# Head norms' squares joined in pairs before they are summed, key roots as two parts, and the second half's x kept unshifted: a hybrid decoder block on one core

## The chip, the cores and the metric

The kernel runs on one core of a Trainium2 chip. The metric is the device time of a run in microseconds; the time of a kernel is the median of its runs. TensorE is called PE, VectorE DVE, ScalarE ACT, GpSimd POOL and SyncE SP, as in the profile.

## The reference, cut to what matters

x has 2048 tokens by 1024 channels, in float32. Twelve heads of 128 channels in three groups (dilations 1, 4 and 16) attend over a banded window of at most 128 earlier keys.

```python
h = rms_norm(x, norm_w) * (1.0 + scale) + shift          # shift, scale, gate from silu(c) @ w_ada + b_ada
a, b, g_conv, q, k, v, g_attn, m_conv, m_attn = split(h @ w_in)
u = depthwise_causal_conv(a * sigmoid(b), conv_w, conv_b)      # 31 taps
y_conv = (silu(layer_norm(u)) * silu(g_conv)) @ w_conv_out
q = rope(rms_norm(q, q_norm_w), positions)               # per head of 128
k = rope(rms_norm(k, k_norm_w), positions)
o = softmax-weighted sum over the three groups of dilated_window_attention(q, k, v)
y_attn = (o * silu(g_attn)) @ w_attn_out
y = sigmoid(m_conv) * y_conv + sigmoid(m_attn) * y_attn
x = x + gate * (y @ w_out)
```

The part that the change touches most is `rms_norm` of the heads: the mean of the squares of each head's 128 channels, its inverse root, and the product with q or k.

## The kernel before, in words

**Products.** The combined projection is done in two halves of 1024 tokens. Each product of two 2 x 2 blocks is formed from seven block products (Strassen's scheme, names A11, S1 to S4 for the activations, B11, T1 to T4 for the weights). Each operand is split into a high and a low part of reduced precision (F32R), and a block product is twelve matmuls of 128 x 512 (`product`, line 311): three for each of four slices of 128 channels.

**Slots.** One block product is one slot. `slots` lists them in order: the values of the first pairs, then the q, k, v quads of seven slots each, then the gates' and the convolution's quads, and all this again for the second half. The first half's q, k, v stage lies at about 100 to 345 us of the profile with the attention trailing it, its gates and convolution at 590 to 1010 us, the second half's q, k, v stage at about 1080 to 1510. Work beside the products hangs on an agenda: `at_slot(s, f, where)` puts it into slot s, at the places "enter", "load", "act", "pe", "vec", "act2", (the products, with "mid" after the sixth of twelve) "tail" and "store", in this order. On PE, DVE, ACT, POOL and SP the order of instructions is the order of the program, so an instruction that waits holds up all behind it on its engine. Weight loads are asked five slots ahead, their splits done three slots ahead (`prepare`, lines 248 and 249; subtractions of weights on POOL, line 243).

**A rotation** (`rotate`) belongs to a pair of heads of q or of k: 12 for q and 12 for k in all, each on two registers `reg[0]` and `reg[1]` (the two halves of the heads' channels, 128 rows, two column halves c of 512 tokens). e4, e5, e6 are the slots of the quad's fifth to seventh product. ACT squares the four pieces (line 588); PE sums each over its channels with four products with the selector `sel`, one in each group of 32 columns of the array (line 601, four calls of `sums`, the two of one c adding up in PSUM); ACT adds eps (line 607); PE turns the rows into columns (line 612); ACT copies 16 columns (line 617); POOL takes the power -0.5 (line 621). For q the roots go into the scores' mask step. For k ACT widens them (line 631, two steps of 128 x 512), PE spreads them by eight products with the identity (line 638), DVE multiplies k by them (line 642), and SP stores (line 647). Meanwhile DVE turns by the positions' angles, twelve steps (lines 658 to 665).

**Attention** (`unit`) runs in units of two blocks of 128 queries, one every second slot, after its q, k, v are stored: scores (line 764), the mask step on DVE (line 776), exponents, transposed probabilities (line 792), values (line 817). The first half's attention waits for the end of the second half's x.

**The second half's x** (`later_load`, `later_scale`, `later_sum`) is normed beside the first half's q, k, v stage: loaded, multiplied by its row roots (DVE, line 1282), scaled and shifted in place (ACT, line 1283), summed in Strassen's combinations (DVE, line 1291), and stored; `quarter_split` (line 183) splits it when the second half starts. How its steps fall on slots is set by `busy`, `room` and `when`.

**The start** (lines 994 to 1200): x's first rows are squared and summed on PE, the modulation is formed from c and w_ada (`ada_mm`, `ada_mod`), `first_part` scales, shifts and splits x, and `angle_steps` works through the positions' angles on DVE.

Of the kernel before, what the change touches and what calls it, by code (L numbers as in the profile page):

```python
# [62 lines left out]
def tile_hybrid_block(  # L63
# [79 lines left out]
    nc.gpsimd.memset(eps, EPS)  # L143
    hpool_c = [tc.tile_pool(name=f"hT{i}", bufs=1, side="right", reuse_waits="tile") for i in range(2)]
# [67 lines left out]
    def rope_open(half):  # L212
        p = opened(rp, pool("rp"))
        rp["cos"], rp["sin"] = (p.tile([P, HS], F32, name=f"{n}{half}") for n in ("cos", "sin"))

# [347 lines left out]
    def turn_v(half, _, u0, g, reg, n, at):  # L563
        s0 = at[6]
# [13 lines left out]
    def rotate(half, which, u0, g, reg, n, at):  # L578
# [12 lines left out]
        turns = []  # L591

        def sums(c, i):
            def f():
                if not turns:
                    box["pr"] = bank("u", f"pss{n}")
                pr, sq = box["pr"], box.pop(("sq", c, i))
                first, done = not turns, c in turns
                turns.append(c)
                for q in range(4):  # L600
                    nc.tensor.matmul(pr[32 * q : 32 * q + 32, P * c : P * c + P], sel, sq[:, P * q : P * q + P],
                                     start=first, stop=done, skip_group_check=True)
            return f
# [5 lines left out]
        def turned():  # L609
            pt = box["pt"] = bank("t", f"prq{n}")  # L610
            for c in range(2):
                nc.tensor.transpose(pt[:, P * c : P * c + P], box["rows"][:, c], ident)

        def more():
            st = box["st"] = rb["p"].tile([P, 32], F32, tag="st", name=f"st{n}", bufs=2)
            got = box["pt"][:, : 2 * P].rearrange("p (c q m) -> p c q m", c=2, q=4)[..., :2]
            nc.scalar.activation(st[:, :16].rearrange("p (c q m) -> p c q m", c=2, q=4), got, AF.Copy)
# [8 lines left out]

        def widen():
            box["wide"] = rp["p"].tile([P, 16, 64], F32, tag="wide", name=f"rw{n}", bufs=1)
            for c in range(2):
                sl = slice(8 * c, 8 * c + 8)  # L630
                nc.scalar.activation(box["wide"][:, sl], box["st"][:, 16 + 8 * c : 24 + 8 * c][:, :, None].to_broadcast([P, 8, 64]), AF.Copy)

        def spread():
            box["rs"] = [bank("tu"[c], f"rs{n}_{c}") for c in range(2)]
            for c in range(2):
                for q in range(4):
                    w = box["wide"][:, 8 * c + 2 * q : 8 * c + 2 * q + 2].rearrange("p m r -> p (m r)")
                    nc.tensor.matmul(box["rs"][c][:, P * q : P * q + P], w, ident, start=True, stop=True)
# [36 lines left out]
        for s, c, i in sq:  # L675
            at_slot(s, square(c, i), "act" if s > e6 else "act2")
            at_slot(max(s, e6 - 1), sums(c, i), "tail")
        ops = rope()
        assert sum(count) == 12
        for d, k in enumerate(count):  # L680
            rope_slots[start + d] = k
            for _ in range(k):
                at_slot(start + d, lambda: next(ops)())
        end = start + len(count)
        at_slot(last, rows, "act")
        at_slot(last, turned, "mid")
        at_slot(last, more, "tail")
        at_slot(last + 1, roots)
# [3 lines left out]
        else:  # L692
            at_slot(last + 2, widen, "act2")
            at_slot(last + 2, spread, "tail")
            for c in range(2):
                for i in range(2):
                    at_slot(last + 3 + c, key_scale(c, i))
            assert last + 3 + 1 >= end - 1
            for i in range(2):
                at_slot(last + 5, store(i), "load")  # L700
# [3 lines left out]
    def unit(half, u, bs, state):  # L704
# [18 lines left out]
        def load():  # L723
# [25 lines left out]
            state["prev"] = own[1]  # L749
            box["q"] = [qk[:, 0, i] for i in range(2)]  # L750
# [106 lines left out]
    wide = su.tile([P, KC, 32], F32, name="wide")  # L857
# [56 lines left out]
    def ada_mm(g, acc, k):  # L914
        for q in range(4):
            nc.tensor.matmul(acc[32 * q : 32 * q + 32, :256], wide[:, k], landed_ada(g, k)[:, q // 2, 256 * (q % 2) : 256 * (q % 2) + 256],
# [25 lines left out]
    def first_part(name, k, t):  # L942
# [59 lines left out]
    nc.vector.tensor_copy(wide, sc[:, :, None].to_broadcast([P, KC, 32]))  # L1002
# [145 lines left out]
    angle_steps(3)  # L1148
# [54 lines left out]
    at_slot(1, lambda: angle_steps(3))  # L1203
# [49 lines left out]
    def later_root():  # L1253
        nc.vector.tensor_tensor(xst1[:, 16:24], xst1[:, :8], xst1[:, 8:16], op=ALU.add)
        rsqrt_cols(xst1[:, 24:32], xst1[:, 16:24], 8, xst1[:, 32:40])

# [22 lines left out]
    def later_scale(k, i):  # L1279
        name, kh, t = LATER[i]  # L1280
        kk, q = 4 * kh + k, xh[name]
        nc.vector.tensor_tensor(q, q, xh["rs"][:, 512 * t : 512 * t + 512], op=ALU.mult)
        nc.scalar.activation(q, q, AF.Identity, scale=mod[:, KC + kk : KC + kk + 1], bias=mod[:, kk : kk + 1])
# [3 lines left out]
    def later_sum(k, n, dst, x0, x1, op):  # L1287
# [3 lines left out]
        nc.vector.tensor_tensor(*q, op=op)  # L1291
# [13 lines left out]
    for w in ((Q, 0), (K, 0), (Q, 1), (K, 1), (Q, 2), (K, 2)):  # L1305
        g = GROUPS[2 * w[1] // NH]
        s6 = slots_of[0, *w][6]
        busy.update(range(s6 + (2 if g == 2 else 0), s6 + (7 if g == 2 else 6)))
# [6 lines left out]
    for k in range(4):  # L1315
# [3 lines left out]
        for args in ((3, "s3", "11", "21", ALU.subtract), (1, "21", "21", "22", ALU.add), (2, "11", "21", "11", ALU.subtract),  # L1319
                     (4, "12", "12", "11", ALU.subtract)):  # L1320
            work.append(lambda k=k, args=args: later_sum(k, *args))
# [3 lines left out]
        when += 2  # L1325
# [48 lines left out]
    for half in range(2):  # L1374
        for pair in range(6):
# [6 lines left out]
            ready = max(k6 + (11 if g == 2 else 10), v6 + 7, free_at[half])  # L1382
# [11 lines left out]
        at_slot(q_end + 6, lambda half=half: conv_open(half), "enter")  # L1394
# [531 lines left out]
```

## Time and profile before

| | |
|---|---|
| median of three runs | 2396.64 us (2391.16 to 2396.83) |
| profiled execution, its own time | 2400.4 us |
| its span, first to last instruction | 2398.6 us |
| PE busy | 2319.5 us (97%) |
| DVE busy | 1751.2 us (73%) |
| ACT and POOL busy | 1093.7 us (46%), 1083.1 us (45%) |
| mean granted TensorE clock | 0.986 |

How to read the profile: busy times are per engine; a line number is a line of the kernel before; "out<-in" names what an instruction writes and reads, numbers of buffers left out; "<-" in brackets names what ended the idle time before an instruction. A full-precision product is recorded as two matmuls, so x16 is eight products. A matmul's duration includes its way through the array, so the distance between starts, 0.23 us for 128 x 512, is what it costs in a run. In a timeline row the first number is the start in us, the second the duration.

### The profile page before, as it was taken

Reading aid. Unit: us, or ns where it says so; the run is one execution under the profiler, and the core shown is the slowest. Engines: PE = TensorE matmul, PEld = TensorE weight load, DVE = VectorE, ACT = ScalarE, POOL = GpSimd, SP = SyncE. Lnnn points to the kernel's source line nnn. Section 1 sums busy time; section 2 is a strip of 40 time slices with the busy share of each in tenths; the row PEclk is TensorE's granted clock in tenths of the full one; section 3 lists DMA queues with packets and bytes.
Section 4 is the critical chain, followed back from the end, with each engine's and each line's share of the span. In section 5 each row is a group of like instructions: output and inputs, shape, how many; then the busy total and the mean of one; then the engine's idle time right before and its main releaser. Section 6 shows DMA issues by size and latency. Waiting matters only on the chain.

```text
span 2398.6 us, 35365 instructions
## 1 busy us (share of the span) xinstructions
PE 2319.5 (97%) x11862; PEld 1892.1 (79%) x11862; DVE 1751.2 (73%) x2902; ACT 1093.7 (46%) x2211; POOL 1083.1 (45%) x841
## 2 busy tenths in 40 slices
PE   6999899999999999999999999999999989999999
PEld 4777678888778888787888887887888877888887
DVE  6878685554999999936656446469999987787644
ACT  4765445455554444554555444653444443332221
POOL 2466454445446778856433333445656630000221
PEclk9999999999999999999999999999999999999999
DMA  7655656576545436643665755755445469866553
GB/s 255 198 184 189 220 178 197 181 217 221 178 157 186 159 134 214 224 132 106 195 191 170 216 170 167 261 161 182 141 136 153 150 226 320 293 232 198 173 165 101
DMA packets 304109, 451.58 MB, mean 188 GB/s; under 512 B 29236, under 2 KB 132788, under 8 KB 303928
## 3 DMA queue, kind: packets, MB, share of 16 engines
q1 hardware_dynamic: 289656, 423.62, 55.8%
q10 hardware_dynamic: 14272, 25.72, 2.9%
q8 instruction: 93, 1.52, 0.3%
q14 instruction: 88, 0.72, 0.1%
HBM read 284.98 MB, written 164.24 MB: 187 GB/s over the span
## 4 chain that ended last, share of the span: by engine, by line
PE 74%; DVE 7%; DMA 3%; ACT 1%; issue 1%; SPq 1%; POOL 0%; ACTq 0%; DVEq 0%; POOLq 0%
PE yc L1537 7%; PE paab L311 6%; PE pak L311 4%; PE pav L311 4%; PE oa L1819 4%; PE paq L311 4%; PE pag_ma_d L311 4%; PE pcab L311 3%; PE po L817 3%; PE ya L1537 3%; PE ps L764 3%; PE pag_mc_d L311 2%; PE pag_g_d L311 2%; PE pck L311 2%; PE pcv L311 2%; PE oc L1819 2%
## 5 line engine op out<-in xcount | busy, mean ns | idle before, releaser
L249 POOL TENSOR_TENSOR slT<-wT,shT 128x512 fp32r<-128x512 f32 x188 | 252.5, 1344 | 332.8 <-ACT shT L248 267.1
L249 POOL TENSOR_TENSOR slB<-wB,shB 128x512 fp32r<-128x512 f32 x142 | 191.9, 1351 | 177.8 <-ACT shB L248 161.6
L248 ACT ACTIVATE shB<-wB 128x512 fp32r<-128x512 f32 x234 | 147.3, 630 | 182.2 <-issue 47.3
L249 POOL TENSOR_TENSOR slT<-wB,shT 128x512 fp32r<-128x512 f32 x98 | 133.5, 1365 | 167.4 <-ACT shT L248 142.4
L248 ACT ACTIVATE shT<-wT 128x512 fp32r<-128x512 f32 x192 | 120.3, 627 | 145.1 <-POOL wT L243 22.6
L371 DVE SCALAR_TENSOR_TENSOR ce<-ut,chan,ce 128x512 f32<-128x512 f32 x240 | 180.1, 750 | 3.7
L400 DVE SCALAR_TENSOR_TENSOR ce<-us,pair_taps,ce 128x512 f32<-128x512 f32 x240 | 179.9, 750 | 2.6
L776 DVE CUSTOM_DVE_ANT_0 sm<-ps,mask,rqq 128x256 f32<-128x256 f32 (+1 forms) x192 | 78.2, 445 | 111.8 <-PE ps L764 81.6
L384 DVE SCALAR_TENSOR_TENSOR cq<-ut,chan,cq 128x512 f32<-128x512 f32 x208 | 155.4, 747 | 0.0
L243 POOL TENSOR_TENSOR wB<-wB,wB 128x512 f32<-128x512 f32 x80 | 111.1, 1389 | 47.3 <-DVE slB L249 40.8
L248 ACT ACTIVATE shT<-wB 128x512 fp32r<-128x512 f32 x120 | 75.2, 627 | 67.7 <-PE paab L311 19.7
L794 DVE COPY pT<-ptp 128x512 f32<-128x512 f32 (+2 forms) x96 | 59.0, 615 | 54.8 <-PE ptp L792 54.5
L137 POOL TENSOR_SCALAR stf<-stf 128x4 f32<-128x4 f32 x4 | 1.8, 460 | 191.6 <-DVE stf L1575 191.6
L249 DVE TENSOR_TENSOR slB<-wB,shB 128x512 fp32r<-128x512 f32 x92 | 74.2, 806 | 18.0 <-ACT shB L248 15.3
L817 PE MATMUL po<-v,pT 128*128 128x128 f32 x560 | 81.9, 277 | 0.7 <-ACT shT L248 0.6
L1747 ACT ACTIVATE yh<-yq 128x512 fp32r<-128x512 f32 x48 | 27.3, 623 | 118.6 <-POOL yq L1741 46.0
L817 PEld LDWEIGHTS po<-v,pT 128*128 128x128 f32 x560 | 75.5, 192 | 7.3 <-issue 1.2
L764 PE MATMUL ps<-qk 128*128 128x128 f32 x512 | 75.6, 275 | 0.8 <-DMA qk<-qk_d 0.8
L764 PEld LDWEIGHTS ps<-qk 128*128 128x128 f32 x512 | 66.2, 192 | 1.1 <-DMA qk<-qk_d 1.0
L783 ACT ACTIVATE sm<-sm,osb 128x256 f32<-128x256 f32 (+1 forms) x128 | 58.5, 460 | 7.4 <-DVE osb L776 3.2
L243 POOL TENSOR_TENSOR wT<-wB,wB 128x512 f32<-128x512 f32 x40 | 56.8, 1420 | 2.0
L243 POOL TENSOR_TENSOR wB<-wB,wT 128x512 f32<-128x512 f32 x40 | 56.8, 1420 | 0.0
(819 smaller groups left out, 7727.8 us busy)
## 6 DMA issues: line engine op xcount, KB each, us to landing
wB<-in_w_in_dram SPq DMA_DIRECT2D x274, 256.0 KB, 4.4
wT<-tT_d SPq DMA_DIRECT2D x152, 256.0 KB, 2.9
tT_d<-wB SPq DMA_DIRECT2D x114, 256.0 KB, 3.7
qk<-qk_d SPq DMA_DIRECT2D x96, 256.0 KB, 4.2
v_d<-vev SPq DMA_DIRECT2D x48, 256.0 KB, 3.3
qk_d<-spare_hi SPq DMA_DIRECT2D x48, 256.0 KB, 4.1
qk_d<-spare_lo SPq DMA_DIRECT2D x48, 256.0 KB, 3.9
v<-v_d SPq DMA_DIRECT2D x96, 128.0 KB, 3.8
```

The source lines that it names most:

```text
L243: nc.gpsimd.tensor_tensor(dst, x0, x1, op=ALU.subtract)
L248: nc.scalar.activation(h, q[name], AF.Copy)
L249: eng.tensor_tensor(l, q[name], h.bitcast(F32), op=ALU.subtract)
L311: nc.tensor.matmul(ps, x, y, start=(first and m == 0), stop=(last and m == 11), skip_group_check=True)
L371: stt(box["e"], e[:, 1 + j : 513 + j], chan[:, cb, 2 * j : 2 * j + 1], box["e"], op0=ALU.mult, op1=ALU.add)
L384: stt(box["o"], o[:, 2 + j : 514 + j], w, psum_o, op0=ALU.mult, op1=ALU.add)
L400: stt(dst, box["both"][:, 1 + j : 513 + j], pair_taps[:, cb, j : j + 1], box["e"], op0=ALU.mult, op1=ALU.subtract if j == 0 else ALU.add)
L764: nc.tensor.matmul(ps[:, c : c + P], box["q"][i], kt, start=True, stop=True)
L776: nc.vector.tensor_tensor_reduce(sm[:, a:z], ps[:, a:z], m[:, 256 - (z - a) :], rq[:, b, u % 2 : u % 2 + 1], 3e38, ALU.add, ALU.min, box[" ...
L817: nc.tensor.matmul(po[:, P * i : P * i + P], box["pT"][:, c : c + P], vt, start=(m == 0), stop=(m == count[i] - 1))
L1537: nc.tensor.matmul(pz, w, xx, start=(m == 0), stop=(m == len(terms) - 1))
L1819: nc.tensor.matmul(ps, y, w, start=(m == 0 and ps.name not in begun), stop=(m == 11 and not more), skip_group_check=True)
```

## The change

- **Squares.** DVE adds the two registers' squares of a column half (`joined`, two per rotation), and PE sums the joined squares: two calls of `sums` per rotation for four. In groups 0 and 1 both calls stand at the tail of e6 + 1, in group 2 (dilation 16) in the middle of e6 + 2. The rope's steps in groups 0 and 1 start one slot later.
- **Turned.** The rows are turned by two products with 8 columns of the identity instead of two transposes, so that only the 16 columns needed come out; `st` has one buffer of 64 columns for two of 32.
- **Key roots.** ACT rounds the 16 roots to a high part (`upper`), DVE forms the low part (`lower`), PE transposes the 32 columns (`turned_back`), DVE multiplies them with a mask `turns4` into 32 rows by 4 by 128 (`widen`), and PE spreads them by two products of 512 columns with 32 rows of `pick`. All four products with k then stand in slot e6 + 7, the spread in e6 + 6 (before: e6 + 4 or 5, the products over two slots).
- **Scores.** In groups 0 and 1 the second block's two score products of 128 columns become one of 256.
- **The second half's x** is scaled and multiplied by its root in one DVE step, and not shifted; the shift comes in where x is summed or split (`by`, `plus`). The loads of the next four slices come one slot later (`when += 3`).
- **The start.** Three angle steps move from before the modulation into slots 0 and 1; every second in-place scaling goes from DVE to ACT; `wide` goes, its use reads `sc` broadcast. Two small reductions on the identity form `turns4` and `pick`'s source.
- **Order.** Attention is ready at k6 + 11 in all groups; the last pair's values turn one slot later, and the convolution's pool opens one slot later.

```diff
+    turns4 = edge_tile[:32, 44:48]
+    nc.vector.tensor_reduce(turns4, ident[:32, :32].rearrange("p (a q m) -> p q a m", a=4, q=4), op=ALU.add, axis=AX.XY)
+    nc.vector.tensor_reduce(edge_tile[:32, 48:52], ident[:32, :32].rearrange("p (c j m) -> p c m j", c=2, m=2), op=ALU.add, axis=AX.X)
...
@@ quarter_split
-        nc.scalar.activation(h, raw, AF.Copy)
-        return eng.tensor_tensor(l, raw, h.bitcast(F32), op=ALU.subtract)
+        plus = {"A11": mod[:, k : k + 1], "A12": mod[:, 4 + k : 5 + k], "A22": mod[:, 4 + k : 5 + k]}.get(name)
+        if plus is not None and eng is nc.gpsimd:
+            eng.tensor_scalar(raw, raw, plus, None, op0=ALU.add)
+            plus = None
+        if plus is None:
+            nc.scalar.activation(h, raw, AF.Copy)
+            eng.tensor_tensor(l, raw, h.bitcast(F32), op=ALU.subtract)
+        else:
+            nc.scalar.activation(h, raw, AF.Identity, scale=1.0, bias=plus)
+            eng.scalar_tensor_tensor(l, raw, plus, h.bitcast(F32), op0=ALU.add, op1=ALU.subtract)
@@ rope_open
+        rp["pick"] = p.tile([P, 2, P], F32R, name=f"pick{half}")
...
@@ rotate
+        def joined(c):
+            def f():
+                sq = box["sq", c, late[c]]
+                tt(sq, sq, box.pop(("sq", c, 1 - late[c])), op=ALU.add)
...
-                pr, sq = box["pr"], box.pop(("sq", c, i))
+                pr, sq = box["pr"], box.pop(("sq", c, late[c]))
                 for q in range(4):
                     nc.tensor.matmul(pr[32 * q : 32 * q + 32, P * c : P * c + P], sel, sq[:, P * q : P * q + P],
-                                     start=first, stop=done, skip_group_check=True)
+                                     start=True, stop=True, skip_group_check=True)
...
-                nc.tensor.transpose(pt[:, P * c : P * c + P], box["rows"][:, c], ident)
+                nc.tensor.matmul(pt[:, 8 * c : 8 * c + 8], box["rows"][:, c], ident.rearrange("p (q r) -> p q r", r=32)[:, :, :2],
+                                 start=True, stop=True)
...
+        def upper():
+            (hi, lo), r = cut()
+            nc.scalar.activation(hi, r, AF.Copy)
+        def lower():
+            (hi, lo), r = cut()
+            tt(lo, r, hi.bitcast(F32), op=ALU.subtract)
+        def turned_back():
+            box["pt"] = bank("t", f"pw{n}")
+            nc.tensor.transpose(box["pt"][:32, :P], box["st"][:, 32:], ident)
         def widen():
-            box["wide"] = rp["p"].tile([P, 16, 64], F32, tag="wide", name=f"rw{n}", bufs=1)
-            for c in range(2):
-                sl = slice(8 * c, 8 * c + 8)
-                nc.scalar.activation(box["wide"][:, sl], box["st"][:, 16 + 8 * c : 24 + 8 * c][:, :, None].to_broadcast([P, 8, 64]), AF.Copy)
+            wide = box["wide"] = rp["p"].tile([P, 4, P], F32R, tag="wide", name=f"rw{n}", bufs=1)
+            tt(wide[:32], box["pt"][:32, None, :P].to_broadcast([32, 4, P]), turns4[:, :, None].to_broadcast([32, 4, P]), op=ALU.mult)
         def spread():
-                for q in range(4):
-                    w = box["wide"][:, 8 * c + 2 * q : 8 * c + 2 * q + 2].rearrange("p m r -> p (m r)")
-                    nc.tensor.matmul(box["rs"][c][:, P * q : P * q + P], w, ident, start=True, stop=True)
+                nc.tensor.matmul(box["rs"][c], rp["pick"][:32, c], box["wide"][:32].rearrange("p q i -> p (q i)"),
+                                 start=True, stop=True)
...
         if g == 2:
-            sq = ((e6 + 1, 0, 0), (e6 + 1, 0, 1), (e6 + 2, 1, 0), (e6 + 2, 1, 1))
-            start, last = e6 + 2, e6 + 3
+            sq = ((e6, 0, 1, "act2"), (e6, 1, 1, "act2"), (e6 + 1, 0, 0, "act"), (e6 + 1, 1, 0, "act2"))
+            joins = ((e6 + 1, "vec"), (e6 + 1, "tail"))
+            added = ((e6 + 2, "mid"), (e6 + 2, "mid"))
         else:
-            sq = ((e4, 0, 0), (e4 + 1, 1, 1), (e6, 0, 1), (e6 + 1, 1, 0))
-            start, last = e6, e6 + 2
+            sq = ((e4, 0, 0, "act2"), (e4 + 1, 1, 1, "act2"), (e6, 0, 1, "act2"), (e6 + 1, 1, 0, "act"))
+            joins = ((e6, "tail"), (e6 + 1, "vec"))
+            added = ((e6 + 1, "tail"), (e6 + 1, "tail"))
+            start = e6 + 1
...
-            at_slot(last + 2, widen, "act2")
-            at_slot(last + 2, spread, "tail")
+            steps = ((5, "act2"), (5, "tail"), (6, "pe"), (6, "act2"), (6, "tail"), (7, "vec")) if g == 2 else (
+                (4, "tail"), (5, "vec"), (5, "tail"), (6, "act2"), (6, "tail"), (7, "vec"))
+            for (d, where), f in zip(steps, (upper, lower, turned_back, widen, spread, lambda: [key_scale(c, i)() for i in range(2) for c in range(2)])):
+                at_slot(e6 + d, f, where)
@@ scores
+                if i and g < 2:
+                    nc.tensor.matmul(ps[:, 2 * P :], box["q"][1], box["k2"], start=True, stop=True)
+                    continue
@@ first_part, t == 0
-            nc.vector.tensor_scalar(x, x, by, plus, op0=ALU.mult, op1=ALU.add)
+            if k % 2:
+                nc.scalar.activation(x, x, AF.Identity, scale=by, bias=plus)
+            else:
+                nc.vector.tensor_scalar(x, x, by, plus, op0=ALU.mult, op1=ALU.add)
@@ the start
-    angle_steps(3)
     ada_mod(0, ada_row(0, acc), "t")
...
-    at_slot(1, lambda: angle_steps(3))
+    at_slot(0, lambda: angle_steps(2), "tail")
+    at_slot(1, lambda: angle_steps(4))
@@ later_scale
-        nc.vector.tensor_tensor(q, q, xh["rs"][:, 512 * t : 512 * t + 512], op=ALU.mult)
-        nc.scalar.activation(q, q, AF.Identity, scale=mod[:, KC + kk : KC + kk + 1], bias=mod[:, kk : kk + 1])
+        stt(q, q, mod[:, KC + kk : KC + kk + 1], xh["rs"][:, 512 * t : 512 * t + 512], ALU.mult, ALU.mult)
...
-        when += 2
+        when += 3
     later_done = when + 1
...
-            ready = max(k6 + (11 if g == 2 else 10), v6 + 7, free_at[half])
+            ready = max(k6 + 11, v6 + 7, free_at[half])
```

More of the change, by code (lines that the diff above doesn't have):

```diff
@@ L214, in rope_open @@
         rp["cos"], rp["sin"] = (p.tile([P, HS], F32, name=f"{n}{half}") for n in ("cos", "sin"))
+        rp["pick"] = p.tile([P, 2, P], F32R, name=f"pick{half}")
+        for c in range(2):
+            nc.vector.tensor_copy(rp["pick"][:32, c].rearrange("p (m r) -> p m r", m=2),
+                                  edge_tile[:32, 48 + 2 * c : 50 + 2 * c][:, :, None].to_broadcast([32, 2, 64]))
     def tables_load(half, g):
@@ L681, in rotate @@
             rope_slots[start + d] = k
-            for _ in range(k):
+            for m in range(k):
                 at_slot(start + d, lambda: next(ops)())
         end = start + len(count)
[L685 to L688, printed above, removed]
+        if g == 2:
+            at_slot(e6 + 2, rows, "tail")
+            for where, f in (("mid", turned), ("tail", more), ("tail", roots)):
+                at_slot(e6 + 3, f, where)
+        else:
+            for where, f in (("act", rows), ("mid", turned), ("tail", more), ("tail", roots)):
+                at_slot(e6 + 2, f, where)
         if which == 0:
@@ L1255, in later_root @@
         rsqrt_cols(xst1[:, 24:32], xst1[:, 16:24], 8, xst1[:, 32:40])
+        tt(sum_of, mod[:, :4], mod[:, 4:8], ALU.add)
+    sum_of = edge_tile[:, 0:4]
     def later_open():
@@ L1307, in tile_hybrid_block @@
         s6 = slots_of[0, *w][6]
-        busy.update(range(s6 + (2 if g == 2 else 0), s6 + (7 if g == 2 else 6)))
+        busy.update(range(s6 + (2 if g == 2 else 1), s6 + 7))
         if w[0] == K:
```

57 lines of the change are left out of this document (31 added, 26 removed).

## The prediction

> **What bounds the kernel now.** I read the page first (busy time and the 40 slices), then the busy time by stage, then the timeline of TensorE around each small product that the change touches, and last the waits of TensorE.
>
> ```profile
> span 2398.6 us, 35365 instructions
> PE 2319.5 (97%) x11862; PEld 1892.1 (79%) x11862; DVE 1751.2 (73%) x2902; ACT 1093.7 (46%) x2211; POOL 1083.1 (45%) x841
> PE   6999899999999999999999999999999989999999
> DVE  6878685554999999936656446469999987787644
> ```
>
> PE (TensorE's products) is busy nearly everywhere, so work taken off it shortens the span, unless another engine sets the pace of that stage. DVE has nines in slices 10 to 16, where the first half's gates and convolution run. The stages:
>
> ```profile
> 100.00:345.00 245.00, 223.33 (x1185) 174.96 (x1184) 184.44 (x221) 129.55 (x231) 138.67 (x89) 0.96 0.62 198
> 590.00:1010.00 420.00, 406.01 (x1907) 336.12 (x1905) 408.75 (x715) 199.58 (x419) 283.58 (x237) 0.99 0.53 178
> 1080.00:1510.00 430.00, 424.40 (x2620) 352.75 (x2618) 250.74 (x471) 211.94 (x485) 171.00 (x122) 1.00 0.59 178
> ```
>
> Columns: window, its length, busy PE, PEld, DVE, ACT, POOL, granted clock, DMA share, GB/s. In the first q/k/v stage (100 to 345 us) PE stands idle 21.7 us at a mean clock of 0.96, beside a DVE busy 75%. In the same stage of the second half (1080 to 1510) PE is the bound outright and DVE is at 58%. Between them (590 to 1010) DVE is at 97%.
>
> **The change part by part.** A small product is priced by what it adds to a run of 512-column products, which start 0.23 us apart: the time from the product in front to the second one behind, less 0.46.
>
> *Sums of squares.* Each call is four products in four column groups.
>
> ```profile
> 140.16 0.39 PE L311 MATMUL pck<-S_hi,slB 128*128 128x512 f32 x1
> 140.47 0.65 PE L601 MATMUL pssk<-sqk,sel 128*32 128x128 f32 x16
> ...
> 141.39 0.40 PE L311 MATMUL pak<-A_lo,shT 128*128 128x512 f32 x1
> ...
> 143.72 0.39 PE L311 MATMUL pak<-A_hi,slT 128*128 128x512 f32 x1
> 144.03 0.42 PE L601 MATMUL pssk<-sqk,sel 128*32 128x128 f32 x8
> ...
> 144.72 0.39 PE L311 MATMUL pbq<-A_lo,shB 128*128 128x512 f32 x1
> ```
>
> Two calls together (x16) cost 141.39 - 140.16 - 0.46 = 0.77 us, one alone (x8) 0.54; so the second call costs 0.23 and going into and out of the column groups about 0.31. In groups 0 and 1 a rotation has two calls together and two alone, 1.85 us; after, two together, 0.77. That is 1.08 by 16 rotations = 17.3 us. In group 2 two pairs of calls become one pair: 0.77 by 8 = 6.2. Sum: 23.4 us less, on PE, on the path. The Trainium skill ("TensorEngine Tiling (Array Packing)", Key Properties) says that a change of the tiling mode drains the engine; by it each entry costs time of its own, and the 0.31 agrees.
>
> *Key roots spread.* Eight full-precision 128-column products of this kind stand undisturbed elsewhere:
>
> ```profile
> 180.13 0.39 PE L311 MATMUL pck<-S_hi,slT 128*128 128x512 f32 x1
> 180.36 1.95 PE L1266 MATMUL rsx<-ident,edge 128*128 128x128 f32 x16
> ...
> 182.38 0.39 PE L311 MATMUL pak<-S_lo,shT 128*128 128x512 f32 x1
> ```
>
> They cost 1.79 us. After: one transpose of 32 columns and two reduced-precision products of 512 columns with 32 rows. The trace has no product with 32 rows. From below: a transpose at 0.11 (next fence) and two steps of 0.23, 0.57. From above: products at the full-precision 0.44 (fence after it), two entries at 0.31, 0.11: 1.6. I take two steps of 0.23 with two entries, 1.2, since the sums row is the nearest that leaves the full array. Gain 0.59 by 12 keys = 7.1 us (2 to 14.7).
>
> *Rows turned.* Two transposes become two full-precision products with 8 columns.
>
> ```profile
> 148.96 0.39 PE L311 MATMUL paq<-S_hi,slT 128*128 128x512 f32 x1
> 149.19 0.38 PE L612 MATMUL prqk<-ident,ssrk 128*128 128x128 f32 x2
> ...
> 149.64 0.39 PE L311 MATMUL paq<-S_lo,shT 128*128 128x512 f32 x1
> ...
> 1992.11 0.40 PE L1537 MATMUL ya<-ai_1h,wal 128*128 128x512 f32 x1
> 1992.34 0.95 PE L1573 MATMUL pc<-ones,red 128*128 128x1 f32 x8
> ...
> 1993.46 0.40 PE L1537 MATMUL ya<-ai_2l,wah 128*128 128x512 f32 x1
> ```
>
> The two transposes cost 0.22. Four products of a single column (x8, as each is recorded twice) cost 0.89: a full-precision product takes two passes of 0.11, however few its columns. Two cost 0.45, so this is a loss of 0.23 by 24 = 5.4 us (0 if the passes hide, 5.4 as taken).
>
> *Scores.* 64 pairs of 128-column products with the same weights become one of 256 columns.
>
> ```profile
> 1774.03 0.40 PE L311 MATMUL pcab<-S_hi,slB 128*128 128x512 f32 x1
> 1774.27 1.02 PE L1443 MATMUL pg<-gate_sum,ones 128*128 128x512 f32 x2
> ...
> 1775.36 0.39 PE L311 MATMUL paab<-A_lo,shT 128*128 128x512 f32 x1
> ```
>
> A full-precision product of 512 columns costs 0.87, so one of 256 is an estimated 0.44; two of 128 cost 1.79 / 4 = 0.45. The columns are paid for, not the instructions: about 1 us (0 to 14, if passes cost 0.11 whatever their width; the 512-column row excludes it).
>
> PE's work: -23.4 - 7.1 + 5.4 - 1 = -26 us.
>
> *Waits for the roots.* The longest waits of PE are for the spread:
>
> ```profile
> PE rsk L638 <- ACT rwk L631: 12.3, 4, 4.9
> ```
>
> ```profile
> 206.57 0.39 PE L311 MATMUL paq<-S_hi,slT 128*128 128x512 f32 x1
> 210.98 3.78 PE L638 MATMUL rsk<-ident,rwk 128*128 128x128 f32 x16 [4.02 <-ACT rwk L631]
> ...
> 214.99 0.63 PE L311 MATMUL pak<-A_lo,shB 128*128 128x512 f32 x1
> 206.89 3.38 POOL L621 TENSOR_TENSOR stk<-stk,mhalf 128x16 f32<-128x16 f32 x1
> 262.01 0.82 ACT L1283 ACTIVATE xl<-xl,mod 128x512 f32<-128x512 f32 x1 [4.41 <-DVE xl L1282]
> ```
>
> Here POOL's power ended at 210.27, ACT widened, and PE, idle for 4 us, came back at about half pace (3.44 us for the eight products instead of 1.70): 214.99 - 206.57 - 1.79 - 0.46 = 6.2 us lost. The row counts 12.3 us of idle time in four places; at the same ratio, 6.2 for 4.0, they lose 19. After, ACT cuts the roots in two and waits for POOL as before, with the next slot's evictions queued behind it, but PE needs the roots one slot (12 steps, 2.8 us) later, which covers this wait but for some 1.6; and the sixteen in-place ACT steps on the second half's x (L1283), behind which ACT waited for DVE, go. I expect 14 of the 19 back. New: two handovers from DVE to PE (the low part, and the masked copy) on each of 12 keys, 0.3 us each by my estimate from a DVE at 75%: 3.6 (0 to 18). Net -10 us (+4 to -19).
>
> *Other engines.* DVE gains 48 joins and 12 masked copies at 0.69 or so, 41 us, of which 14 in the first stage (184 busy of 245 becomes 198) and the rest mostly where DVE is at 58%: hidden, as long as DVE isn't late (rivals). ACT loses 24 widenings and 16 in-place steps. POOL gets three additions behind the end of the first half. SP waits for the four key products in one slot instead of two; its weight loads are asked five slots ahead, which covers that. The three-way scalar forms on the second half's x cost as much as the plain ones. The reductions at the very start run while DVE idles for positions. All nothing.
>
> *The start.* Three angle steps leave DVE's queue ahead of the modulation:
>
> ```profile
> 24.17 1.22 DVE L966 SCALAR_TENSOR_TENSOR spare_hi<-spare_lo,spare_hi 128x1024 f32<-128x1024 f32 x1
> ...
> 29.73 0.15 DVE L930 TENSOR_TENSOR mod<-pt_ada,cols 128x8 f32<-128x8 f32 x1
> ```
>
> PE's transpose was out by 26.5, so the modulation and all behind it comes 3 us sooner; half of the in-place steps go to ACT beside DVE, which saves another 1 or 2. The angle steps come back ahead of the second row sums: 3 by 1.22, where DVE idled 2.3. Net -3 (-6 to +2).
>
> *Attention one slot group later.* The loads of the second half's x get one slot more each, and the first half's attention, which waits for their end, starts four slots later by the schedule's arithmetic (slot 81 for 77). So two units of group 0, some 5 us of DVE each, move from before the convolution into the stage where DVE is at 97% (11 us idle in 420). At the end of that stage PE already waits for DVE. I take +4 (0 to +10).
>
> Sum: -26 - 10 - 3 + 4 = -35 us. The profiled execution took 2400.4; 2400.4 - 35 = 2365, and the median shown lies 3.8 lower, so **2361**.
>
> **Rivals.**
> *A, more than the sum.* All waits for roots go, the two spread products cost 0.57, and the start gives its 6: -26 - 7.6 - 19 - 6 = -58.6, 2338. For it: the waits hang on one slot. Against: POOL's 3.4 us power is still in the chain.
>
> *B, DVE sets the pace and nothing is left.* In the first stage DVE goes to 81% and holds the quads back, so that its 8 us of gain (8 rotations, 4 keys) are lost, the waits grow by 4 in place of shrinking, and the 97% stage takes the full 10: -26 + 8 + 4 + 10 - 3 = -7, 2390. For it: DVE steps stretch beside POOL.
>
> ```profile
> L664 DVE TENSOR_TENSOR spare_hi<-spare_hi x24: 676/689/1823, 127.0 to 1483.4; 128x512 f32<-128x512 f32 x24
> ```
>
> The same addition takes 0.69 in the median and up to 1.82. The Trainium skill ("GPSIMD Engine Reference", Key points) says that GpSimd shares its SBUF interfaces with VectorE and collides with DVE instructions of two SBUF inputs. By it the joins, which are such, cost up to 1.8 each next to POOL; the row agrees.
>
> *C, slower: the join makes PE wait.* In groups 0 and 1 the last square, its join and the sums fall into one slot; behind the join DVE has the rope's first two steps and a weight split, behind the sums PE has all its products.
>
> ```profile
> 145.29 0.63 ACT L588 ACTIVATE sqk<-spare_lo 128x512 f32<-128x512 f32 x1
> 147.34 0.16 PEld L601 LDWEIGHTS pssk<-sqk,sel 128*32 128x32 f32 x8 [0.35 <-ACT xn L1251]
> ```
>
> From the square's end (145.92) to the sums 1.42 us are left: enough for a join of 0.69, not for one of 1.82, nor for one behind another step. It decides when the mean wait over 24 rotations passes 35 / 24 = 1.5 us. At 2 us, with as much again for the clock as at 206 us, 16 rotations lose 64: -35 + 64 = +29, 2426. Against: in the second half DVE idles 42%.
>
> **How the numbers follow.** The forecast 0.70 (2342 to 2385 its own), A 0.12, B 0.10, C 0.08. A tells nothing from no change within 0.3%, 2389.4 to 2403.8, which is about what a measurement here can tell. Faster: the forecast, A and a third of B, 0.85; same: the rest of B and the edge of C, 0.08; slower 0.07. The range reaches from A's end to B's: 2336 to 2392.
>
> **What would show it.** Sums recorded as x16 once per rotation, in all 384 rows instead of 768 (the group's count); spread rows with 32 rows and 512 columns adding 1.2 us, the turned rows 0.45; score products of 256 columns recorded at 0.22 each, the attention stage no shorter per unit; the wait of PE for the spread below 4 us in sum; first scores after the last step on x. The prediction is wrong if PE waits for the joins (sums on DVE), if the first stage stays as long as before, or if PE's wait at the end of the first half (1004 to 1010 us) grows by 10.

## The result, and the profile after

The changed kernel took 2425.6 us in the median (2420.2 to 2432.1), the kernel before beside it 2394.2 (2391.2 to 2396.8): a ratio of 1.0133, with 1.0103 to 1.0162 as its 95% interval. It is 1.3% slower, about 32 us, where 2361 had been forecast. The profiled execution took 2425.99 us, its span 2423.9.

First the page of the changed kernel for the whole span, then busy times by stretch. Of the stretches, the first two rows and the last are the changed kernel; the third is the kernel before, from 345 to 590 us, which has not been shown yet:

```profile
span 2423.9 us, 34180 instructions
PE 2302.4 (95%) x11242; PEld 1874.7 (77%) x11242; DVE 1820.0 (75%) x2976; ACT 1074.2 (44%) x2187; POOL 1090.0 (45%) x844
```
```profile
100.00:345.00 245.00, 211.09 (x995) 163.92 (x994) 206.81 (x232) 108.62 (x195) 136.73 (x86) 0.94 0.58 188
345.00:590.00 245.00, 232.82 (x1232) 192.41 (x1230) 139.38 (x291) 115.77 (x299) 114.10 (x80) 0.97 0.64 198
```
```profile
345.00:590.00 245.00, 244.09 (x1426) 203.84 (x1425) 129.34 (x299) 125.47 (x323) 115.94 (x89) 1.00 0.67 205
```
```profile
1080.00:1510.00 430.00, 414.34 (x2307) 343.27 (x2306) 271.67 (x478) 205.56 (x464) 169.52 (x122) 0.99 0.57 170
```

PE is busy 17 us less than before (2302 for 2319.5) in a span 25 us longer, so it stands idle 121.5 us instead of 79.1. From 100 to 345 us its idle time went from 21.7 to 33.9 us and its clock from 0.96 to 0.94; from 1080 to 1510 us, where PE had been the bound outright, idle time went from 5.6 to 15.7. The first half's q, k, v products don't end at 345 us, as the description of the kernel before has it, but run on to about 520 us: from 345 to 590 us idle time went from 0.9 to 12.2. These three stretches hold 34 of the 42 us of new idle time. The waits of PE that are new or larger:

```profile
PE pwk L658 <- DVE stk L654: 23.2, 11, 5.6
PE pssk L618 <- DVE sqk L609: 7.6, 7, 2.2
PE pssq L618 <- DVE sqq L609: 7.5, 3, 4.7
PE rsk L667 <- DVE rwk L662: 6.5, 6, 1.9
```

Columns: who waits, for what, us in total, times, longest. L618 is `sums`, waiting for the joins (L609). The same call in the kernel before waited for squares, 3.1 us:

```profile
PE pssk L601 <- ACT sqk L588: 1.8, 2, 1.4
...
PE pssq L601 <- ACT sqq L588: 1.3, 1, 1.3
```

L658 is `turned_back`, which waits for DVE's `lower` (L654); L667 is `spread`, which waits for the masked copy (L662). These two are 29.7 us, where the kernel before had 12.3 for the widened roots.

One key shows how the 23.2 us come about. First ACT, then DVE, then PE, in the changed kernel (L650 is `upper`):

```profile
1128.20 0.24 ACT L650 ACTIVATE stk<-stk 128x16 fp32r<-128x16 f32 x1
```
```profile
1128.46 1.10 DVE L526 TENSOR_TENSOR spare_hi<-spare_hi,pcq 128x512 f32<-128x512 f32 x1 [2.32 <-ACT stk L650]
1129.48 1.39 DVE L692 SCALAR_TENSOR_TENSOR spare_lo<-spare_lo,hw,sin 128x512 f32<-128x512 f32 x1
1130.80 0.74 DVE L693 SCALAR_TENSOR_TENSOR spare_lo<-spare_lo,hw,cos 128x512 f32<-128x512 f32 x1
1131.46 1.23 DVE L654 TENSOR_TENSOR stk<-stk 128x16 fp32r<-128x16 f32 x1
```
```profile
1129.61 0.39 PE L326 MATMUL pak<-A_hi,slB 128*128 128x512 f32 x1
1132.83 0.37 PE L658 MATMUL pwk<-ident,stk 128*32 128x128 f32 x1 [2.83 <-DVE stk L654]
1132.86 0.78 PE L326 MATMUL pcq<-S_hi,shB 128*128 128x512 f32 x1
...
1135.99 0.51 PE L326 MATMUL pcq<-S_lo,shB 128*128 128x512 f32 x1
```

ACT had cut off the upper part by 1128.44. DVE had all it needed for the lower one, but takes its queue in order: an eviction's addition and two rope steps first (L526, L692, L693), 3 us. Just before, it had stood idle for 2.32 us: it was late by its order, not by its load. Then the subtraction itself, 16 columns, took 1.23 us instead of 0.16. PE stood still 2.83 us, and its next seven steps are 0.45 us apart instead of 0.23, another 1.5 us.

### The profile page after: what moved, and what is told of

Its sections match the earlier page's. It is cut to its first block, busy times and chain, and to the rows that moved or that the text cites. A ratio compares the mean times of both kernels' runs of the same rounds, so it can differ in the third digit from the quotient of the medians.

```text
span 2423.9 us, 34180 instructions
## 1 busy us (share of the span) xinstructions
PE 2302.4 (95%) x11242; PEld 1874.7 (77%) x11242; DVE 1820.0 (75%) x2976; ACT 1074.2 (44%) x2187; POOL 1090.0 (45%) x844
## 4 chain that ended last, share of the span: by engine, by line
PE 61%; DVE 9%; DMA 3%; issue 2%; POOL 1%; ACT 1%; SPq 0%; DVEq 0%; POOLq 0%; ACTq 0%
PE yc L1587 7%; PE paab L326 6%; PE oa L1869 4%; PE pag_ma_d L326 3%; PE pcab L326 3%; PE ya L1587 3%; PE pav L326 2%; PE paq L326 2%; PE pag_mc_d L326 2%; PE pak L326 2%; PE pag_g_d L326 2%; PE po L861 2%; PE oc L1869 2%; PE pbab L326 1%; PE pcg_ma_d L326 1%
## 5 line engine op out<-in xcount | busy, mean ns | idle before, releaser
L264 POOL TENSOR_TENSOR slT<-wT,shT 128x512 fp32r<-128x512 f32 x188 | 257.8, 1372 | 317.5 <-ACT shT L263 305.3
L836 PE MATMUL ptp<-ident,sm 128*128 128x128 f32 x332 | 52.7, 275 | 5.3 <-DVE stm L820 4.1
L836 PEld LDWEIGHTS ptp<-ident,sm 128*128 128x128 f32 x332 | 41.2, 140 | 20.1 <-issue 6.6
```

The lines of the kernel that those rows point to most:

```text
L264: eng.tensor_tensor(l, q[name], h.bitcast(F32), op=ALU.subtract)
L836: nc.tensor.transpose(pt[:, c : c + P], box["sm"][:, c : c + P], ident)
```

## The experiments

All ratios are against the kernel before on the same chip, with 95% intervals; 0.1% is 2.4 us. Theory Q, later split into P and L, says that PE waits for small DVE steps placed late in an in-order queue (P: putting them first is enough; L: the way is too long whatever the order); theory D, that DVE simply has too much work.

**1. The key roots as before, all else as changed.** The four products with k stay in slot e6 + 7; `widen` on ACT and eight products, `at_slot(e6 + 4 (+1 in group 2), widen, "act2")`, `spread` at that slot's end.

> The changed kernel with one part undone: the key roots are widened on ACT and spread by eight 128-column products, in the slots of the kernel before; the joins, the new start and the later attention stay. Theory Q (the loss is TensorE standing still for small DVE steps that lie behind rope steps in DVE's in-order queue): the two waits of PE for DVE at the key roots, 29.7 us of idle time in the changed kernel, go, and some 5 us of half clock behind them; the eight products cost 0.59 us more on each of 12 keys (+7), and the wait for ACT and POOL that the kernel before had there comes back (+12): 2425 - 35 + 19 = 2409, range 2400 to 2416. Theory D (rival: DVE has simply more work than its stages can hold, wherever it is put): DVE loses only 12 x 0.85 = 10 us of work here, PE gains 7, and the time stays at 2420 to 2430.

Measured: 2404.9 us, 1.0033 (1.0021 to 1.0045), 1.0% or 24 us below the changed kernel. PE's wait there:

```profile
PE rsk L667 <- ACT rwk L660: 3.7, 4, 1.7
```

The key roots' new way alone carries most of the loss, though its products are cheaper. That is in Q's range, and D's 2420 to 2430 is missed; but 10 us of DVE's work left with the new way, so the test of order against load is run 9.

**2. Only `lower` moved.**

```
-  (4, "tail"), (5, "vec"), (5, "tail"), (6, "act2"), ...
+  (4, "tail"), (5, "act"), (5, "tail"), (6, "act2"), ...
```

> The changed kernel with one DVE instruction moved: in groups 0 and 1 the subtraction that gives the low part of the key roots (0.16 us) stands first in DVE's queue of its slot, ahead of the two rope steps and the weight split, instead of behind them. Nothing else differs. Theory Q: PE's wait for it falls from 23.2 us to 8 or less (group 2 keeps its place), with some 4 us of half clock: 2425 - 19 = 2406, range 2399 to 2413. Theory D: the same DVE work in another order gives the wait to the rope steps or the evictions behind, 2420 to 2430. A third way, POOL's power sets it: DVE then stands waiting for ACT's upper part at the head of the slot and PE waits for evictions instead, 2425 to 2435.

Measured: 2425.8 us, 1.0118 (1.0094 to 1.0142): no gain to be told. PE's waits:

```profile
PE pwk L658 <- DVE stk L654: 14.9, 6, 6.9
PE rsk L667 <- DVE rwk L662: 12.7, 8, 2.8
```

The first wait fell by 8.3 us and the second grew by 6.2: with its low part sooner, PE came to the spread sooner and stood there, since the masked copy also lay behind rope steps. Q's number missed, and the time lies in D's range and in the third way's. The third way is not seen in the trace: PE's longest wait for an eviction at the q, k, v quads (`pck`) is 3.8 us in both. What Q says of the queue was not yet refuted, since two steps of the way lie in it.

**3. No joins: four calls of sums.** Each square summed by its own call at the places of before (group 2: in the middle of e6+1 and e6+2).

> The changed kernel with another part undone: no joins on DVE; each of the four squares of a rotation is summed by its own call on PE (four column groups), in group 0 and 1 at the places of the kernel before. Theory Q: the 15.1 us that PE waits for joins go, and 3 to 5 us of half clock with them, while the calls cost 1.08 us on 16 rotations and 0.77 on 8 more (+23): 2425 - 19 + 23 = 2429, within 0.3% of the changed kernel (2422 to 2436). Theory D: 48 joins, 34 us or more of DVE's time, leave, so the key roots' subtraction comes sooner too: 2425 - 15 - 20 + 23 = 2413 or less (2400 to 2416).

Measured: 2445.7 us, 1.0201 (1.0172 to 1.0230), 0.7% or 16 us slower than the changed kernel. The joins are a gain as they stand. Both theories missed: Q had all of the wait there go, but without joins PE still waited 11.0 us at the sums' calls; the rest of the miss was not followed.

**4. Two slots between the loads of the second half's x.** `when += 3` becomes `when += 2`.

> The changed kernel with one number changed: the loads of the second half's x get two slots between channels again instead of three, so that the first half's attention may start some four slots sooner, as in the kernel before. Theory A (the later attention is one of the losses): the delay against the kernel before grows by 9 us between 729 and 754 us of the span in the changed kernel, and that goes: 2416, range 2411 to 2420. Theory N (the 9 us there are the delay of before, handed on, or DVE's own pace): 2422 to 2429.

Measured: 2416.0 us, 1.0091 (1.0060 to 1.0122), 0.4% or 10 us below the changed kernel, as theory A has it. The stretch 680 to 760 us of the kernel before, the changed kernel and this one, in this order:

```profile
680.00:760.00 80.00, 77.25 (x370) 64.44 (x371) 76.79 (x154) 36.03 (x82) 44.02 (x40) 0.96 0.51 169
```
```profile
680.00:760.00 80.00, 72.25 (x371) 59.95 (x370) 79.63 (x185) 38.85 (x104) 41.05 (x38) 0.98 0.56 180
```
```profile
680.00:760.00 80.00, 75.28 (x363) 61.96 (x362) 77.69 (x160) 36.24 (x86) 42.39 (x38) 0.96 0.52 168
```

The third number is PE, the fifth DVE. With the later attention, DVE is busy 79.63 of 80 us there and PE falls to 72.25: late attention work runs into the convolution's stage (12 of the attention's mask steps in this stretch, for 6 in the kernel before).

**5. Both DVE steps first, groups 0 and 1.** As in 2, and the masked copy from `(6, "act2")` to `(6, "act")`.

> The changed kernel with both DVE steps of the key roots' way put first in DVE's queue of their slots, in groups 0 and 1: the low part as in the run before (which gave no time: PE's wait for it fell by 8 us, its wait for the masked copy grew by 6), and now the masked copy too. Group 2 keeps its places. Theory P (both steps must be ahead, one alone only moves the wait to the next): the 12.7 us of waits for the masked copy fall to 4 or less, the 14.9 us left for the low part are group 2's: 2426 - 11 = 2415, range 2409 to 2420. Theory L (the way is too long whatever the order: POOL, ACT, DVE, PE, DVE, PE, with DVE late by its other work): 2421 to 2430.

Measured: 2409.7 us, 1.0088 (1.0068 to 1.0107): 0.45% or 11 us below the changed kernel, where moving one step had given nothing. PE no longer waits for the masked copy; left is

```profile
PE pwk L658 <- DVE stk L654: 13.2, 6, 5.2
```

of which 11.9 are group 2's. P holds in groups 0 and 1.

**6 to 8. Giving time instead of order.** In 6 the whole way ends a slot later (transposed back in the middle of e6+6, spread at the end of e6+7, scaled in e6+8, v turned a slot later); 7 adds the sums half a slot later, 8 also the loads two slots apart. In these three most keys are stored only behind an addition of the quad after next into the same scratch tile (in run 6, for one key, the addition ends at 178.40 us and the store is issued at 178.43), so these keys hold other data; the work is the same.

> The changed kernel with the key roots' way given time: the transpose back stands in the middle of the slot e6+6, the masked copy first in DVE's queue of e6+7, the spread behind the products of e6+7 and the scaling of the key in e6+8, a slot (2.8 us) later than in the changed kernel, for every group; the turning of v moves by one slot, since it takes the same bank. No work is added or taken away. Theories P and L both: the 29.7 us of waits go, with some 5 us of half clock: 2425 - 33 = 2392, range 2384 to 2400. Theory D (DVE has more work than its stages hold): the waits move to evictions and to the turning of v, 2412 to 2428.

> The kernel with the key roots' way a slot later, and the joins given time too: in groups 0 and 1 the eight sums products stand in the middle of the slot after the join instead of at the end of its own (1.4 us later), with the rows, their turn and the roots following a slot later, as group 2 has it already. If the joins' waits are lateness alone (15.1 us of idle time of PE, with 3 us of half clock): 13 to 18 us below the run with the key roots' way a slot later, some 2376 (2370 to 2386). If DVE's pace is what is short: the waits come back at the key roots, less than 5 us.

> All three together: the key roots' way a slot later, the joins' sums half a slot later, and the loads of the second half's x two slots apart as in the kernel before (alone it gave 10 us). If the three losses lie apart from each other they add: 2425 - 33 - 15 - 10 = 2367, range 2358 to 2380, below both kernels. If they share DVE's time, 2380 to 2395.

Measured: 2427.1 (1.0149, 1.0134 to 1.0164), 2440.6 (1.0206, 1.0190 to 1.0221) and 2435.5 us (1.0184, 1.0168 to 1.0199): nothing, and worse. P and L missed in run 6, and both ranges missed in runs 7 and 8. Run 6 lies in D's range (2412 to 2428), and D had the waits move to evictions and to the turning of v, as they do; but the evictions wait for a store, not for DVE. ACT's wait of run 6, then PE's of run 7:

```profile
ACT spare_lo L524 <- DMA qk_d<-spare_lo: 57.1, 8, 9.3
```
```profile
PE prqq L629 <- ACT ssrq L624: 21.3, 4, 8.0
```

A key that is stored a slot later holds its scratch tiles a slot longer. The eviction that wants the tile waits for that store's DMA, a wait of ACT that the changed kernel does not have, and behind it in ACT's queue wait the rows whose turn PE has next. A later end of the way costs more than it gives; its steps have to come sooner.

**9 and 10. Group 2 first too, then the loads.** The order of 5, and in group 2 `(5, "act"), (5, "act"), (5, "tail"), (6, "act"), (6, "tail"), (7, "vec")`; 10 adds the edit of 4.

> The run with both DVE steps of the key roots' way first in their slots in groups 0 and 1 (2410 us), and the same now for group 2: upper and lower part first in ACT's and DVE's queues of e6+5, the transpose back at that slot's end, the masked copy first in DVE's queue of e6+6. Theory P (lateness in DVE's in-order queue): the 13.2 us that PE still waits for the low part fall to 3 or less, with 3 us of half clock: 2410 - 13 = 2397, range 2391 to 2404. Theory L (in group 2 the roots come from POOL one slot later, so the queue's head waits for POOL and the evictions behind it come late): 2406 to 2416.

> The same with the loads of the second half's x two slots apart, as in the kernel before. If the two losses lie apart, they add: 2397 - 10 = 2387, range 2380 to 2395, that is some 38 us below the changed kernel. If the earlier attention takes DVE's time where the key roots' steps need it, 2395 to 2407.

Measured: 2398.0 us, 1.0018 (1.0003 to 1.0033), and 2385.0 us, 0.9973 (0.9958 to 0.9988). Both came out within a few us of what P gave. Run 9's waits at the key roots, and the key shown above in it:

```profile
PE pwk L658 <- DVE stk L654: 5.3, 5, 1.5
PE rsk L667 <- DVE rwk L662: 5.3, 3, 2.9
```
```profile
1120.09 1.11 DVE L526 TENSOR_TENSOR spare_hi<-spare_hi,pcq 128x512 f32<-128x512 f32 x1 [2.29 <-ACT stk L650]
1121.11 0.87 DVE L654 TENSOR_TENSOR stk<-stk 128x16 fp32r<-128x16 f32 x1
1121.91 0.74 DVE L692 SCALAR_TENSOR_TENSOR spare_lo<-spare_lo,hw,sin 128x512 f32<-128x512 f32 x1
```

The same steps in another order: the waits are 10.6 us instead of 29.7, and the time 1.15% (28 us) less. No work was added or removed (DVE is busy 1821.1 us for 1820.0). So it was order, not DVE's load, that cost the changed kernel most; and run 10 is faster than the kernel before.

**11. The joins alone.** The kernel before with only the squares, joins and sums of the change.

> The kernel before with one part of the change alone: the squares are added in pairs on DVE and summed by two calls instead of four, with the squares, joins and sums where the changed kernel has them; the key roots, the rows' turn, the scores, the start and the second half's x stay as before. Price by the changed kernel's trace: 23 us less of products on PE, against some 4 us that PE waits longer for joins than it waited for squares: 2394 - 19 = 2375, range 2368 to 2384. The rival (48 joins on DVE push the rope steps, weight splits and evictions back and eat the gain): 2388 to 2400.

Measured: 2378.0 us, 0.9936 (0.9915 to 0.9958): 15 us faster than before. PE waits for joins 12.7 us, where it had waited 3.1 for squares:

```profile
PE pssk L603 <- DVE sqk L594: 7.0, 5, 2.7
PE pssq L603 <- DVE sqq L594: 5.7, 3, 2.6
```

**12. The angle steps back.** `angle_steps(3)` ahead of the modulation again, three instead of six in the first two slots.

> The changed kernel with the three angle steps back in DVE's queue ahead of the modulation and three instead of six in the first two slots, as in the kernel before. The changed kernel had gained 4.6 us at 98 us of its span and was 2 us behind at 111, with PE waiting for weight splits of DVE. If the angle steps are what was given back there: the start comes 3 us later, the wait at 105 to 109 goes, and the end is the same, 2422 to 2429. If they cost more than they gave: 2417 to 2422. If the forecast's -3 us held: 2427 to 2431.

Measured: 2422.1 us, 1.0117 (1.0099 to 1.0134), not to be told from the changed kernel. Moving these steps only exchanges one wait for another. The changed kernel's rows, then run 12's:

```profile
PE xm L940 <- DVE xrow L936: 3.8, 2, 3.2
...
PE pC L326 <- ACT A_hi L991: 2.4, 2, 2.1
```
```profile
PE pC L326 <- ACT A_hi L991: 5.0, 2, 3.7
...
PE xm L940 <- DVE xrow L936: 1.1, 2, 0.6
```

The changed kernel waits 2.6 us less at the first products and 2.7 more at the second row sums. A new wait of 3.6 us for a weight split (`pcq`, near 105 us) stands in both. In the changed kernel's trace DVE works without a pause from 92 to 109 us there; the last three steps ahead of the split take 5.2 us beside a busy POOL, where they took 2.0 in the kernel before. So PE, coming sooner, met a DVE that did not.

**13 and 14. Which further part pays.** Run 13: run 11 with the key roots as two parts, placed first as in 9. Run 14: run 11 with the rows turned by eight-column products.

> The kernel before with two parts of the change: the joins (alone: 2378 us), and the key roots as two parts with their steps first in ACT's and DVE's queues of their slots, for every group. Start, rows' turn, scores and the second half's x as before. Theory P (the spread is worth what its products say, once nothing waits for it): 12 x 0.59 = 7 us less of products on PE, and about as much of PE's wait for the widened roots (7.5) goes as the two new handovers cost (6 to 10): 2378 - 7 = 2371, range 2365 to 2377. Rival (two handovers more cost what the products save, wherever they stand): 2376 to 2386.

> The kernel before with the joins and the rows turned by full-precision products with eight columns instead of transposes. By their rows they add 0.45 us to a run of products where the transposes added 0.22: 24 rotations by 0.23 = 5.4 us: 2378 + 5 = 2383, range 2380 to 2387. If the pair lies in a wait that PE has anyway: 2376 to 2380.

Measured: 2376.2 us, 0.9926 (0.9902 to 0.9950), and 2389.0 us, 0.9986 (0.9973 to 0.9999). Run 13 cannot be told from the joins alone, and both of its ranges hold 2376.2; its waits at the key roots are

```profile
PE pwk L650 <- DVE stk L646: 5.7, 6, 2.2
...
PE rsk L659 <- DVE rwk L654: 2.2, 2, 1.5
```

7.9 us, as much as the old way's 7.5 in run 11. The two traces show more than the medians: PE is busy 10.5 us less than in run 11 (2285.7 for 2296.2) and idle 7.2 us more, 2.9 of it at the joins. So the cheaper spreads gave about what their products say, and waits elsewhere took most of it back. The turn by products costs 0.5%, some 12 us (5 to 19), outside both ranges of run 14: PE is busy 5.5 us longer than in run 11 (2301.7), as the products say, and idle 6.4 us longer.

## Why the prediction was wrong

*The prices on PE were right.* The timeline of the changed kernel, as the prediction read that of before (from the product in front to the second behind, less 0.46):

```profile
126.24 0.39 PE L326 MATMUL pbk<-A_hi,slB 128*128 128x512 f32 x1
126.56 0.64 PE L618 MATMUL pssq<-sqq,sel 128*32 128x128 f32 x16
...
127.47 0.40 PE L326 MATMUL pak<-S_lo,shT 128*128 128x512 f32 x1
...
128.41 0.39 PE L326 MATMUL pak<-S_hi,slT 128*128 128x512 f32 x1
128.65 0.51 PE L629 MATMUL prqq<-ident,ssrq 128*128 128x8 f32 x4
...
129.32 0.39 PE L326 MATMUL pak<-S_lo,shT 128*128 128x512 f32 x1
...
1137.02 0.39 PE L326 MATMUL pcq<-S_hi,slB 128*128 128x512 f32 x1
1137.34 0.73 PE L667 MATMUL rsk<-rwk,pick 32*128 32x512 f32 x2
...
1138.33 0.39 PE L326 MATMUL paq<-A_lo,shT 128*128 128x512 f32 x1
```

Sums 0.77 once per rotation (forecast 0.77), the turn 0.45 (0.45), the spread 0.85; its transpose, read in run 9 where nothing holds it up (from 167.95 to 168.52 us), 0.11. The last two together are 0.96 where 1.2 was taken. What failed lies beside PE.

*The waits for roots: the step that failed.* The prediction took 14 us off these waits and priced the two new handovers at 0.3 us each "from a DVE at 75%", 3.6 in all. (Two on each of 12 keys at 0.3 are 7.2, not 3.6; the slip is small beside what follows.) It asked for less than 4 us of waiting at the spread. It counted DVE's load and not what stands ahead of each step in DVE's queue; with the way that the change moved, the wait was 29.7 us where 12.3 had stood, and the whole part (forecast: spread -7, waits -10) cost 24 us by run 1, and order alone gave back 28 in run 9. That is 41 of the 67 us between the forecast -35 and the measured +32. Its bounds for the handovers, 0 to 18, did not reach the 29.7 us of idle time, let alone the clock behind it.

*The joins: mechanism right, size off.* Forecast -23, with the joins hidden; alone they gave -15, since PE waits 12.7 us for them. Rival C, "the join makes PE wait", named this place but asked for 1.5 us in every rotation; the mean over 24 was 0.6. The result met C's 2426 for another reason: the wait that decides is at the key roots. The longest of the joins' waits, 4.7 us up to 233.86, is no lateness of DVE: ahead of the join its addition waits for a key's store, as in runs 6 to 8:

```profile
232.27 1.02 DVE L526 TENSOR_TENSOR spare_lo<-s1k,pbk 128x512 f32<-128x512 f32 x1 [4.86 <-DMA qk_d<-spare_lo]
```

*Rows turned:* +5.4 forecast, some 12 by run 14, with PE's own price as forecast; the other half is idle time, spread over several waits, whose cause was not followed further.

*The start:* -3 forecast; the gain came and went. The same product (`paq`) starts at 93.79 us where it had started at 98.38, and the next but a few at 112.86 instead of 110.89, behind the two waits told of under run 12. Of this part only the angle steps were run alone.

*Attention later:* +4 (0 to 10) forecast, +10 by run 4 and +11 between runs 9 and 10, at the upper bound. The prediction named the stage and took the middle of a range whose row, DVE at 97%, spoke for its end. It looked for the loss at the stage's end; PE's wait there did not grow (5.3 us for 5.6), and the loss shows near 730 to 755 us.

By the runs: joins -15, key roots +24, turn +12, attention +10, angle steps 0, sum +31; measured +32. The parts were not all taken from the same kernel, so that they add so well is in part luck. The scores, the unshifted x and the rest of the start were not run alone.

*Rival B* (DVE sets the pace) is refuted in its main point: with DVE as busy as in the changed kernel, run 9 is 28 us faster. Its 10 us for the later attention came out.

## What to carry to other kernels

Price a handover by what stands ahead of the step in its engine's queue at that moment, not by that engine's busy share; where a chain crosses the same engine twice, both steps must come first, for moving one only hands the wait to the next. Before a chain is given more slots, look at what buffer it holds: a later store kept a tile that the next eviction needed, and the wait came back elsewhere. And of several small savings on the bound engine, run each alone: here one of them was worth more than the whole.

## What the runs showed of the hardware

A short wait of PE can halve the clock behind it, and a longer one need not. Three stretches of the changed kernel, each right behind a wait of PE; the third number from the right is the granted clock:

```profile
329.10:332.10 3.00, 3.00 (x13) 2.49 (x14) 3.00 (x4) 0.16 (x1) 1.79 (x2) 1.00 0.00 0
446.20:449.20 3.00, 3.00 (x9) 2.29 (x10) 1.84 (x4) 0.00 (x0) 0.00 (x0) 0.59 0.67 255
1132.80:1136.30 3.50, 3.47 (x9) 2.84 (x10) 1.77 (x3) 0.00 (x0) 0.00 (x0) 0.51 0.00 0
```

Behind 3.76 us of idle time (ending at 329.10) the clock stayed full; behind 1.91 us (ending at 446.20) it was 0.59, behind 2.83 us (ending at 1132.83) 0.51. These are no exceptions: of the 14 waits of 1.4 us or longer in the two q/k/v stages, ten (1.51 to 5.59 us) were followed by 3 us at a mean clock of 0.50 to 0.71, four (1.69, 1.72, 2.90 and 3.76 us) by 3 us at full clock. The Trainium skill ("TensorE: Matmul & The Clock Gate", Part 1: The HAM clock gate) warns of idle gaps above about 3.4 us, one window of a counter that runs freely. Six of the ten waits that cost clock here were shorter than that, and one longer cost nothing, so the length alone does not tell in this kernel; that the place in time matters as well would fit a free-running window, but no run here tests it.

The subtraction on 16 columns shows what a neighbour does to a small DVE step:

```profile
L654 DVE TENSOR_TENSOR stk<-stk x12: 160/168/1233, 164.9 to 1503.4; 128x16 fp32r<-128x16 f32 x12
```

Minimum, median and maximum in ns: at 1131.46 us it took 1.23 us, beside a weight split that POOL ran from 1131.36 to 1132.65. Two others of the twelve, at 355.41 and 1246.79 us, also fell beside a subtraction on POOL and took 1.23 us; all three ended within 0.04 us of POOL's step. The other nine, with POOL idle, took 0.16 or 0.17.
